# The first projections of a hybrid attention block: unused products ahead of the loads, gains inside the split of x, first weights on another queue, squares later

## The chip, the cores and the metric

One core of one Trainium2 chip. The metric is the device time of one execution in microseconds. A time of a kernel is the median of several executions; the profile is one further execution, recorded by the hardware profiler.

## The reference

One layer over 512 tokens of width 1024, all in float32, cut here to what the change touches:

```python
h = rms_norm(x, attn_norm)            # x * rsqrt(mean(x^2) + eps) * gain
proj = h @ w_in                       # q, k, v of attention A; cq, ckv, k_pe of attention B
sb_q, sb_k, sb_v, cq, ckv, k_pe = split(proj)
sb = stick_breaking_attention(sb_q, sb_k, sb_v)
q  = rms_norm(cq, cq_norm) @ w_uq
kv = rms_norm(ckv, ckv_norm) @ w_ukv
...                                   # attention B, output projection, PEER layer
```

cq has 384 columns, ckv 256; both are the "latents". The factor rsqrt(mean(x^2) + eps) belongs to a token, so the kernel multiplies x by the gain alone before the products and puts the factor on the products afterwards.

## The kernel before

Every float32 product is made of three fast ones: each operand is split into a high half (rounded to the float32r format by a copy on ScalarE) and a low half (the rest, by a subtraction on VectorE); high x high, high x low and low x high are summed in PSUM. `split` (lines 98 to 109) makes the halves, `mm3` (111 to 114) the three products, `copy_act` (93) is the copy on ScalarE. A weight tile of 128 columns is loaded raw, 512 KB on SP's queue (`raw_load`, line 117, three buffers), and split into two buffers of each half (`wparts`, 129).

x lies transposed: eight pieces xs of 128 rows by 512 tokens, 256 KB each. A projection of one weight tile (`project`, 304) is 8 pieces x 3 = 24 products of 512 columns into one of five PSUM banks.

The order of the work. A planner orders each engine's instructions by priority and by simulated times; `keep` holds instructions to the order written, `high_priority` moves some ahead. At the front two strings of steps are written by hand. ORD0 (line 62) is the order of the loads on SP: x0, the first weight tile w0, x1, x2, w1, x3 to x7, then the positions and a row of constants; the gains come before them (line 264). ORD1 (line 63) is the order of the steps on ScalarE, VectorE and GpSimd: for a piece k, gk is the multiplication by the gain on VectorE into a buffer xg (line 280), hk the high half hh on ScalarE (282), lk the low half hl on VectorE (284), sk a square of the raw piece on ScalarE (287) and its sum on GpSimd (`ssum`, 141 to 145); whk and wlk are the halves of weight tile k (291 and 293).

Behind these stand the tables of sines and cosines (295), the sum of squares over the partitions by a product with ones, psq (296), the token factor rs (`rsqrt`, 147 to 159: VectorE, twice ScalarE, three times VectorE), and its transposed column rcol (298 to 302). `lowrank` (310 to 331) does a latent: for each weight tile the projection, the multiplication by rs (318), a square and its sum; then two products with ones (323, 324: the sum of the earlier squares and the last square by itself), the latent's own factor, the multiplication by it (329) and a split. It runs for cq (tiles 0 to 2), then for ckv (tiles 3 and 4). After them come the value columns (337 to 357): two halves j of eight pieces kk, each piece a load of 136 KB, a split into one of four pairs of buffers (wvh, wvl), and 12 products of 272 columns into four PSUM banks pv of the same five; then the projections of q and k, the up-projections, and the attention heads.

Of the kernel before, what the change touches and what calls it, by code (L numbers as in the profile page):

```python
# [12 lines left out]
F32 = mybir.dt.float32  # L13
F32R = mybir.dt.float32r
BF16 = mybir.dt.bfloat16
# [8 lines left out]
P = 128  # L24
# [37 lines left out]
ORD0 = "x0 w0 x1 x2 w1 x3 x4 x5 x6 x7 t".split()  # L62
ORD1 = "g0 h0 l0 wh0 g1 h1 wl0 l1 s0 g2 s1 h2 g3 wh1 l2 h3 s2 g4 wl1 l3 h4 s3 g5 l4 h5 s4 g6 l5 h6 s5 g7 l6 h7 s6 l7 s7".split()
# [18 lines left out]
def hybrid_block(ctx: ExitStack, tc: tile.TileContext, A, out, out2, dbg=None, stop=None):  # L82
# [169 lines left out]
    with ExitStack() as pr:  # L252
# [10 lines left out]
        with tc.high_priority(offset=5 * AHEAD):  # L263
            nc.sync.dma_start(gains, A["gains"])
# [10 lines left out]
        wm, xg = {}, {}  # L275
        for step in ORD1:
            what, k = step[:-1], int(step[-1])
            if what == "g":
                xg[k] = pp.tile([P, S], F32, name="xg", tag="xg", bufs=2)
                keep(nc.vector.tensor_scalar(xg[k], xs[k], g_attn[:, k:k + 1], None, op0=OP.mult))  # L280
            elif what == "h":
                keep(copy_act(hh[:, k], xg[k]))
            elif what == "l":
                keep(nc.vector.tensor_sub(hl[:, k], xg[k], hh[:, k].bitcast(F32)))
# [10 lines left out]
        tables(pp, rows, posi)()  # L295
        nc.tensor.matmul(psq, ones, sqs, start=True, stop=True)
        rs = rsqrt(pp, psq, D, "x", [P, S])
        ptr = pz.tile([P, S], F32, name="ptr", tag="z1")
        for b in range(NB):
            nc.tensor.transpose(ptr[:, b * P:(b + 1) * P], rs[:, b * P:(b + 1) * P], ident)  # L300
        rcol = pp.tile([P, NB], F32, name="rcol")
        nc.vector.tensor_copy(rcol, ptr[:, ::P])
# [7 lines left out]
        def lowrank(first, n, width, gain, name):  # L310

            raw = pp.tile([P, n, S], F32, name=f"{name}_raw", tag="lr_raw", bufs=1)
            pv = pz.tile([P, S], F32, name=f"{name}_v", tag="z2")
            sqs = pp.tile([P, S], F32, name="sqs", tag="sqs", bufs=1)
            for m in range(n):
                w = wm[first + m] if first + m in wm else wload(A["wm"][first + m], KD, P, f"wm{first + m}")
                ps = project(w, f"{name}{m}")
                nc.vector.tensor_mul(raw[:, m], ps, rs)
                sq = pp.tile([P, S], F32, name="sq", tag="sq", bufs=2)
                nc.scalar.activation(sq, raw[:, m], AF.Square)  # L320
                if m < n - 1:
                    ssum(sqs, sq, m)
# [836 lines left out]
```

## Time and profile before

| | |
|---|---|
| runs of the kernel | 1634.97, 1636.81, 1643.74 us, median 1636.81 |
| profiled execution | 1636.4 us, span of its trace 1634.7 us |
| instructions | 24317 |
| busy: TensorE products, weight loads | 1543.7 us (94%), 1436.5 us (88%) |
| busy: VectorE, ScalarE, GpSimd | 1306.7 us (80%), 718.9 us (44%), 751.7 us (46%) |

PE is TensorE's products and PEld its weight loads, which overlap them; DVE is VectorE, ACT ScalarE, POOL GpSimd, SP the engine whose queue issues most loads. Times count from the start of the span. A line number is one of the kernel before; a helper's line stands for all who call it. In the rows, names such as `hl<-xg,hh` say what is written from what, and the bracket behind an instruction how long its engine stood idle before it and what ended that.

### The profile page before, as it was taken

The page shows a single profiled execution, that of the slowest core. Times are in us where ns is not written, and L with a number is a line of the kernel's source. Part 1 is how long each engine was busy: PE and PEld are TensorE (multiplying, and loading weights), DVE is VectorE, ACT ScalarE, POOL GpSimd, SP SyncE. Part 2 cuts the span into 40 slices and gives each one's busy share as a digit, 9 for nine tenths or more (in the row PEclk, how much of TensorE's full clock was granted, in tenths as well). Part 3 has the DMA queues.
Part 4 walks back from the last instruction along what each step waited for, and adds up shares of the span by engine and source line. Part 5 has one row for each costly group of instructions (what it writes and reads, how often), then busy time and mean ns, then how long its engine had stood idle before and what let it go on. Part 6 is the DMA issues. An engine that isn't in the chain of part 4 may idle for free.

```text
span 1634.7 us, 24317 instructions
## 1 busy us (share of the span) xinstructions
PE 1543.7 (94%) x8983; PEld 1436.5 (88%) x8983; DVE 1306.7 (80%) x2469; ACT 718.9 (44%) x1055; POOL 751.7 (46%) x655
## 2 busy tenths in 40 slices
PE   7998987979899999999999999989999998999996
PEld 4886665759899989989899999989999988999996
DVE  7557998889989899797857676778888888866667
ACT  5434775344444446666653333333333332333331
POOL 3003122434666741211136565655556677745454
PEclk9999998989899999999999999999999999999998
DMA  4330002423455567989899998999999999888776
GB/s 135 96 100 2 1 15 77 116 77 110 159 164 168 161 206 238 313 276 288 273 323 325 313 317 309 314 319 376 347 368 355 360 389 370 313 246 249 252 242 234
DMA packets 146551, 379.96 MB, mean 232 GB/s; under 512 B 11376, under 2 KB 64624, under 8 KB 146432
## 3 DMA queue, kind: packets, MB, share of 16 engines
q1 hardware_dynamic: 109568, 244.18, 44.7%
q0 software_dynamic: 36864, 134.23, 23.2%
q8 instruction: 70, 1.15, 0.3%
q14 instruction: 49, 0.40, 0.1%
HBM read 336.95 MB, written 41.42 MB: 231 GB/s over the span
## 4 chain that ended last, share of the span: by engine, by line
PE 54%; DVE 18%; DMA 14%; POOL 6%; issue 5%; ACT 3%; DVEq 0%; SPq 0%; ACTq 0%; POOLq 0%
PE pacc L113 9%; PE pacc L114 9%; PE pacc L112 9%; DMA row<-u,eidx 7%; PE psu L112 4%; PE psu L114 4%; PE psu L113 4%; POOL row L786 3%; DMA row<-v,eidx 3%; DMA u_r<-ut 3%; POOL tok L826 2%; PE pg L1037 2%; DVE u_l L106 2%; PE psx L113 1%; PE psx L114 1%
## 5 line engine op out<-in xcount | busy, mean ns | idle before, releaser
L113 PE MATMUL pacc<-cl,v_h 128*128 128x384 f32 x1024 | 345.3, 337 | 11.8 <-DVE cl L106 11.8
L112 PE MATMUL psu<-h2h,u_h 128*128 128x384 f32 x1024 | 349.9, 342 | 0.0
L114 PE MATMUL psu<-h2h,u_l 128*128 128x384 f32 x1024 | 345.7, 338 | 3.9 <-DVE u_l L106 3.9
L112 PE MATMUL pacc<-ch,v_h 128*128 128x384 f32 x1024 | 342.9, 336 | 1.9 <-ACT ch L94 1.9
L113 PE MATMUL psu<-h2l,u_h 128*128 128x384 f32 x1024 | 344.5, 336 | 0.0
L114 PE MATMUL pacc<-ch,v_l 128*128 128x384 f32 x1024 | 344.4, 336 | 0.0
L94 ACT ACTIVATE v_h<-v_r 128x1024 fp32r<-128x1024 f32 x128 | 135.9, 1062 | 330.6 <-PE pacc L113 224.8
L786 POOL DMA_INDIRECT row<-v,eidx x128 | 241.2, 1885 | 24.2 <-issue 24.0
L94 ACT ACTIVATE u_h<-u_r 128x1024 fp32r<-128x1024 f32 x128 | 135.6, 1059 | 228.1 <-PE psu L113 112.0
L106 DVE TENSOR_TENSOR v_l<-v_r,v_h 128x1024 fp32r<-128x1024 f32 x128 | 156.6, 1224 | 88.6 <-ACT v_h L94 87.4
L792 DVE CUSTOM_DVE_ANT_0 row<-row,h2n 128x1024 f32<-128x1024 f32 x128 | 158.1, 1241 | 67.4 <-DMA row<-u,eidx 66.7
L113 PEld LDWEIGHTS pacc<-cl,v_h 128*128 128x128 f32 x1024 | 194.1, 190 | 13.6 <-DVE cl L106 13.4
L114 PEld LDWEIGHTS psu<-h2h,u_l 128*128 128x128 f32 x1024 | 193.7, 189 | 5.6 <-DVE u_l L106 5.6
L112 PEld LDWEIGHTS pacc<-ch,v_h 128*128 128x128 f32 x1024 | 193.1, 189 | 2.2 <-ACT ch L94 2.2
L112 PEld LDWEIGHTS psu<-h2h,u_h 128*128 128x128 f32 x1024 | 194.1, 190 | 1.0 <-issue 0.5
L113 PEld LDWEIGHTS psu<-h2l,u_h 128*128 128x128 f32 x1024 | 194.1, 190 | 0.3
L114 PEld LDWEIGHTS pacc<-ch,v_l 128*128 128x128 f32 x1024 | 194.2, 190 | 0.0
L800 DVE SCALAR_TENSOR_TENSOR acc<-row,coef,acc 128x1024 f32<-128x1024 f32 x128 | 163.9, 1280 | 23.6 <-DMA row<-v,eidx 23.0
L826 POOL COPY tok<-u_l 1x1 f32<-1x1 f32 x90 | 56.8, 632 | 262.7 <-DVE u_l L106 262.5
L786 POOL DMA_INDIRECT row<-u,eidx x128 | 160.4, 1253 | 32.0 <-issue 25.2
L826 POOL COPY tok<-v_l 1x1 f32<-1x1 f32 x125 | 80.6, 645 | 197.1 <-DVE v_l L106 197.0
L106 DVE TENSOR_TENSOR u_l<-u_r,u_h 128x1024 fp32r<-128x1024 f32 x96 | 117.3, 1222 | 39.7 <-ACT u_h L94 34.3
(372 smaller groups left out, 2736.8 us busy)
## 6 DMA issues: line engine op xcount, KB each, us to landing
u_r<-ut SPq DMA_DIRECT2D x128, 512.0 KB
v_r<-v SPq DMA_DIRECT2D x128, 512.0 KB
gd<-gbuf SPq DMA_DIRECT2D x12, 2048.0 KB
gr<-gd SPq DMA_DIRECT2D x32, 768.0 KB
pd<-p SPq DMA_DIRECT2D x18, 768.0 KB
pr<-pd SPq DMA_DIRECT2D x18, 768.0 KB
wq_r<-wq SPq DMA_DIRECT2D x16, 512.0 KB
wqk_r<-wqk SPq DMA_DIRECT2D x8, 512.0 KB
```

Source lines behind the costliest of these rows:

```text
L94: return nc.scalar.activation(o, i, AF.Copy, scale=scale)
L106: b = nc.vector.tensor_sub(lo, src, hi.bitcast(F32))
L112: nc.tensor.matmul(ps, wh, xh, start=start, stop=False)
L113: nc.tensor.matmul(ps, wh, xl, start=False, stop=False)
L114: nc.tensor.matmul(ps, wl, xh, start=False, stop=stop)
L786: tc.keep_in_program_order(nc.gpsimd.indirect_dma_start(out=row, out_offset=None, in_=table, in_offset=bass.IndirectOffsetOnAxis(ap=eidx[: ...
L792: tc.keep_in_program_order(nc.vector.tensor_tensor_reduce(row, row, h2n, 1.0, 0.0, OP.mult, OP.add, pre[:, s:s + 1]))
L800: tc.keep_in_program_order(nc.vector.scalar_tensor_tensor(acc, row, coef[:, s:s + 1], acc, op0=OP.mult, op1=OP.add))
L826: tc.keep_in_program_order(nc.gpsimd.tensor_copy(tok, after[0:1, 0:1].bitcast(F32)))
L1037: nc.tensor.matmul(pg[:, u], ebf[:, t], egf[k][:, t], start=(k == 0), stop=(k == 1))
```

## The change

The loads of the gains and of the first weight tile go to ScalarE's queue, the tile in two halves of 256 KB. Thirteen products of a zeroed bf16 tile (`idle`, cleared on GpSimd) are written ahead of the projections; their PSUM tile `warm` is not read. The pass gk is gone: the high half is a copy with the gain as its scale, the low half one instruction that multiplies by the gain and subtracts. The first weight tile is split by halves. The squares of x come later in the order. The five projections of the latents are written before the parts that use rs: tiles 0 to 2, tables, psq, rs, then `lowrank_raw` of cq, tiles 3 and 4, the transposes, `lowrank_raw` of ckv; the rest of each latent's norm is written inside the value loop, before its pieces 1 and 6. Each latent's squares are all summed on GpSimd, with one product with ones for each latent.

```diff
--- before.py
+++ after.py
@@ -59,8 +59,9 @@
 EM0 = "ss0 lh0".split()
 EM = "lm0 ss0 lh1 lo-1 sw0 lw0 so0".split()
 ZB = 2
-ORD0 = "x0 w0 x1 x2 w1 x3 x4 x5 x6 x7 t".split()
-ORD1 = "g0 h0 l0 wh0 g1 h1 wl0 l1 s0 g2 s1 h2 g3 wh1 l2 h3 s2 g4 wl1 l3 h4 s3 g5 l4 h5 s4 g6 l5 h6 s5 g7 l6 h7 s6 l7 s7".split()
+ORD0 = "x0 x1 x2 w1 x3 x4 x5 x6 x7 t".split()
+ORD1 = "h0 wg0 l0 wg1 h1 wm0 l1 h2 wm1 l2 h3 l3 wh1 h4 wl1 l4 s0 h5 l5 s1 h6 l6 s2 h7 l7 s3 s4 s5 s6 s7".split()
+WARM = 13
 POOLQ = (1, 1)
 POOLU = range(0, 32)
 
@@ -261,7 +262,11 @@
         posi = pp.tile([P, NB], I32, name="posi")
         raws = {}
         with tc.high_priority(offset=5 * AHEAD):
-            nc.sync.dma_start(gains, A["gains"])
+
+            raws[0] = ws.tile([P, KD * P], F32, name="wm0_r", tag="wr", bufs=3)
+            nc.scalar.dma_start(gains, A["gains"])
+            for half in range(2):
+                nc.scalar.dma_start(raws[0][:, 512 * half:512 * half + 512], A["wm"][0][:, 4 * half:4 * half + 4])
             for step in ORD0:
                 if step == "t":
                     nc.sync.dma_start(posi, A["pos"])
@@ -272,16 +277,25 @@
                     nc.sync.dma_start(xs[int(step[1])], A["xT"][:, int(step[1])])
         psq = pz.tile([P, S], F32, name="psq", tag="z0")
         sqs = pp.tile([P, S], F32, name="sqs", tag="sqs", bufs=1)
-        wm, xg = {}, {}
+
+        idle = pp.tile([P, S], BF16, name="idle")
+        nc.gpsimd.memset(idle, 0.0)
+        warm = pz.tile([P, S], F32, name="warm", tag="z2")
+        for k in range(WARM):
+            nc.tensor.matmul(warm, idle[:, 0:P], idle, start=True, stop=True)
+        wm = {0: wparts(KD, P, "wm0")}
         for step in ORD1:
             what, k = step[:-1], int(step[-1])
-            if what == "g":
-                xg[k] = pp.tile([P, S], F32, name="xg", tag="xg", bufs=2)
-                keep(nc.vector.tensor_scalar(xg[k], xs[k], g_attn[:, k:k + 1], None, op0=OP.mult))
-            elif what == "h":
-                keep(copy_act(hh[:, k], xg[k]))
+            half = slice(512 * k, 512 * k + 512)
+            if what == "h":
+                keep(copy_act(hh[:, k], xs[k], scale=g_attn[:, k:k + 1]))
             elif what == "l":
-                keep(nc.vector.tensor_sub(hl[:, k], xg[k], hh[:, k].bitcast(F32)))
+                keep(nc.vector.scalar_tensor_tensor(hl[:, k], xs[k], g_attn[:, k:k + 1], hh[:, k].bitcast(F32),
+                                                    op0=OP.mult, op1=OP.subtract))
+            elif what == "wg":
+                keep(copy_act(wm[0][0][:, half], raws[0][:, half]))
+            elif what == "wm":
+                keep(nc.vector.tensor_sub(wm[0][1][:, half], raws[0][:, half], wm[0][0][:, half].bitcast(F32)))
             elif what == "s":
                 sq = pp.tile([P, S], F32, name="sq", tag="sq", bufs=2)
                 keep(nc.scalar.activation(sq, xs[k], AF.Square))
@@ -292,14 +306,6 @@
             else:
                 keep(nc.vector.tensor_sub(wm[k][1], raws[k], wm[k][0].bitcast(F32)))
         wm = {k: wm3d(w, P) for k, w in wm.items()}
-        tables(pp, rows, posi)()
-        nc.tensor.matmul(psq, ones, sqs, start=True, stop=True)
-        rs = rsqrt(pp, psq, D, "x", [P, S])
-        ptr = pz.tile([P, S], F32, name="ptr", tag="z1")
-        for b in range(NB):
-            nc.tensor.transpose(ptr[:, b * P:(b + 1) * P], rs[:, b * P:(b + 1) * P], ident)
-        rcol = pp.tile([P, NB], F32, name="rcol")
-        nc.vector.tensor_copy(rcol, ptr[:, ::P])
 
         def project(w, name):
             ps = pm.tile([P, S], F32, name=f"ps_{name}", tag="mm")
@@ -307,21 +313,22 @@
                 mm3(ps, w[0][:, kk], w[1][:, kk], hh[:, kk], hl[:, kk], kk == 0, kk == KD - 1)
             return ps
 
-        def lowrank(first, n, width, gain, name):
-
-            raw = pp.tile([P, n, S], F32, name=f"{name}_raw", tag="lr_raw", bufs=1)
-            pv = pz.tile([P, S], F32, name=f"{name}_v", tag="z2")
-            sqs = pp.tile([P, S], F32, name="sqs", tag="sqs", bufs=1)
+        def lowrank_raw(pss, name):
+
+            n = len(pss)
+            raw = pp.tile([P, n, S], F32, name=f"{name}_raw")
+            sqs = pp.tile([P, S], F32, name=f"sqs{name}")
             for m in range(n):
-                w = wm[first + m] if first + m in wm else wload(A["wm"][first + m], KD, P, f"wm{first + m}")
-                ps = project(w, f"{name}{m}")
-                nc.vector.tensor_mul(raw[:, m], ps, rs)
+                nc.vector.tensor_mul(raw[:, m], pss[m], rs)
                 sq = pp.tile([P, S], F32, name="sq", tag="sq", bufs=2)
                 nc.scalar.activation(sq, raw[:, m], AF.Square)
-                if m < n - 1:
-                    ssum(sqs, sq, m)
-            nc.tensor.matmul(pv, ones, sqs, start=True, stop=False)
-            nc.tensor.matmul(pv, ones, sq, start=False, stop=True)
+                ssum(sqs, sq, m)
+            return raw, sqs
+
+        def lowrank(raw, sqs, n, width, gain, name):
+
+            pv = pz.tile([P, S], F32, name=f"{name}_v", tag="z2")
+            nc.tensor.matmul(pv, ones, sqs, start=True, stop=True)
             r = rsqrt(pp, pv, width, name, [P, S])
             hi = lp.tile([P, n, S], F32R, name=f"{name}_h")
             lo = lp.tile([P, n, S], F32R, name=f"{name}_l")
@@ -330,8 +337,18 @@
                 split(hi[:, m], lo[:, m], raw[:, m])
             return hi, lo
 
-        cq = lowrank(0, 3, 384, g_cq, "cq")
-        ckv = lowrank(3, 2, 256, g_ckv, "ckv")
+        pss = [project(wm[m] if m in wm else wload(A["wm"][m], KD, P, f"wm{m}"), f"c{m}") for m in range(3)]
+        tables(pp, rows, posi)()
+        nc.tensor.matmul(psq, ones, sqs, start=True, stop=True)
+        rs = rsqrt(pp, psq, D, "x", [P, S])
+        cq = lowrank_raw(pss, "cq")
+        pss = [project(wload(A["wm"][m], KD, P, f"wm{m}"), f"c{m}") for m in (3, 4)]
+        ptr = pz.tile([P, S], F32, name="ptr", tag="z1")
+        for b in range(NB):
+            nc.tensor.transpose(ptr[:, b * P:(b + 1) * P], rs[:, b * P:(b + 1) * P], ident)
+        rcol = pp.tile([P, NB], F32, name="rcol")
+        nc.vector.tensor_copy(rcol, ptr[:, ::P])
+        ckv = lowrank_raw(pss, "ckv")
 
 
         with ExitStack() as wv_:
@@ -344,6 +361,11 @@
                     wvl = vp.tile([P, 272], F32R, name=f"wvl{j}{kk}", tag="wvl")
                     split(wvh, wvl, raw_load(A["wv"][:, kk, js], 272, f"wv{j}{kk}"))
                     st, sp = kk == 0, kk == KD - 1
+
+                    if (j, kk) == (0, 1):
+                        cq = lowrank(*cq, 3, 384, g_cq, "cq")
+                    if (j, kk) == (0, 6):
+                        ckv = lowrank(*ckv, 2, 256, g_ckv, "ckv")
                     for b in range(NB):
                         bs = slice(b * P, (b + 1) * P)
                         nc.tensor.matmul(pv[b], hh[:, kk, bs], wvh, start=st, stop=False)
```

## Rows read from the trace of the kernel before

**Rows 1.** The page, busy time: engine, busy us (share), instructions.
```profile
PE 1543.7 (94%) x8983; PEld 1436.5 (88%) x8983; DVE 1306.7 (80%) x2469; ACT 718.9 (44%) x1055; POOL 751.7 (46%) x655
```

**Rows 2.** Busy time by stage: length; PE, PEld, DVE, ACT, POOL (records); clock, DMA share, GB/s.
```profile
7.00:21.00 14.00, 11.89 (x24) 7.14 (x25) 11.81 (x18) 7.95 (x14) 7.67 (x6) 1.00 0.71 250
...
21.00:36.20 15.20, 13.41 (x57) 9.73 (x56) 13.85 (x30) 9.34 (x15) 4.23 (x3) 1.00 0.10 28
...
36.20:50.40 14.20, 12.87 (x53) 9.67 (x52) 11.16 (x18) 5.96 (x10) 2.33 (x2) 1.00 0.14 40
...
50.40:76.80 26.40, 26.21 (x195) 24.77 (x195) 12.58 (x23) 11.59 (x24) 0.61 (x1) 1.00 0.38 108
...
76.80:130.00 53.20, 53.20 (x245) 44.42 (x244) 29.48 (x45) 20.55 (x36) 2.86 (x5) 1.00 0.28 92
```

**Rows 3.** The chain of waits, 0 to 30 us: start us, us, what.
```profile
3.62 7.64 DMA xs<-xT
...
13.29 2.31 DVE wm_l L293
...
22.57 1.77 DVE hl L284
...
27.16 1.23 DVE wm_l L106
```

**Rows 4.** The timeline of PE: start us, us, engine, line, operation [idle before].
```profile
6.98 0.79 PE L112 MATMUL ps_cq<-hh,wm_h 128*128 128x512 f32 x1 [6.98 <-ACT wm_h L94]
...
20.06 0.63 PE L114 MATMUL ps_cq<-hh,wm_l 128*128 128x512 f32 x1
...
20.48 0.63 PE L112 MATMUL ps_cq<-hh,wm_h 128*128 128x512 f32 x1
...
29.70 0.39 PE L112 MATMUL ps_cq<-hh,wm_h 128*128 128x512 f32 x1
...
33.56 0.39 PE L114 MATMUL ps_cq<-hh,wm_l 128*128 128x512 f32 x1
...
39.96 1.13 PE L323 MATMUL cq_v<-sqs,ones 128*128 128x512 f32 x2 [1.33 <-POOL sqs L145]
...
40.92 1.02 PE L324 MATMUL cq_v<-sq,ones 128*128 128x512 f32 x2
...
50.44 0.28 PE L349 MATMUL pv<-wvh,hh 128*128 128x272 f32 x1
```

**Rows 5.** Groups by line, 0 to 50 us: what xcount | busy us, mean ns | idle.
```profile
L145 POOL TENSOR_TENSOR sqs<-sqs,sq 128x512 f32<-128x512 f32 x8 | 12.7, 1582 | 6.2 <-ACT sq L287 5.0 <-ACT sq L320 0.9
...
L284 DVE TENSOR_TENSOR hl<-xg,hh 128x512 fp32r<-128x512 f32 x8 | 8.7, 1093 | 0.7 <-ACT hh L94 0.7
...
L94 ACT ACTIVATE wm_h<-wm_r 128x1024 fp32r<-128x1024 f32 x5 | 5.3, 1056 | 2.4 <-PE ps_cq L113 2.2
...
L94 ACT ACTIVATE hh<-xg 128x512 fp32r<-128x512 f32 x8 | 5.0, 630 | 9.1 <-DVE xg L280 9.1
...
L280 DVE TENSOR_SCALAR xg<-xs,gains 128x512 f32<-128x512 f32 x8 | 4.8, 600 | 5.6 <-DMA xs<-xT 5.4
```

**Rows 6.** The timeline of the first 5 us: ACT, SP's queue, DVE.
```profile
0.81 1.28 ACT L94 ACT_TABLE_LOAD   x1 [0.81 <-PEq L1148]
...
1.26 0.42 SPq L272 DMA_DIRECT2D xs<-xT  x1
...
4.66 0.49 DVE L280 TENSOR_SCALAR xg<-xs,gains 128x512 f32<-128x512 f32 x1 [3.33 <-DMA xs<-xT]
```

**Rows 7.** Busy time around one pause of PE, columns as in the second group.
```profile
151.10:154.40 3.30, 0.02 (x1) 0.00 (x0) 2.59 (x7) 0.91 (x3) 1.71 (x3) 0.99 0.00 0
...
154.50:161.10 6.60, 5.81 (x13) 2.03 (x14) 5.49 (x14) 2.01 (x4) 0.00 (x0) 0.50 0.03 6
```

**Rows 8.** The waits, 0 to 80 us: who for whom: us, times, longest.
```profile
ACT wvh L94 <- PE pv L350: 4.8, 5, 1.1
```

**Rows 9.** The timeline of DVE: the last low halves of the first norm.
```profile
48.21 1.89 DVE L106 TENSOR_TENSOR cq_l<-cq_raw,cq_h 128x512 fp32r<-128x512 f32 x3
```

## The prediction

> **What bounds the kernel now.** I began with the busy times: TensorE is busy 94% of the span [rows 1], so time can be won only where TensorE stands idle or runs slowly. The busy time by stage says where. From 50.4 to 130 us TensorE is full, 26.21 of 26.40 us and 53.20 of 53.20, while the other engines are not [rows 2]; ScalarE's splits of the value weights even wait for TensorE to release their buffers [rows 8]. Whatever is won before 50 us therefore passes through this stretch as a plain shift. Before 50 us TensorE has gaps, and in 7 to 21 us it retires only 24 products in 14 us [rows 2].
>
> The chain of waits then names what holds TensorE in those first 30 us. It is the fourth piece of x until 11.36 us, and from there VectorE: the second tile's low halves, the last low half of x, the third tile's low halves [rows 3]. VectorE is slow there in two ways. It multiplies x by the gains in a pass of its own, eight times 0.600 us, and its eight low halves of x take 1.093 us on the mean [rows 5]. A pair of low weight halves takes 2.31 us at 13.29 but 1.23 us at 27.16, when GpSimd's sums are over [rows 3]; those sums are 1.58 us each [rows 5]. I read the stretching as a price of GpSimd running beside VectorE.
>
> The timeline of PE adds the clock. At 20 us two products start 0.42 us apart, from 29.70 to 33.56 seventeen steps take 3.86 us, 0.227 each [rows 4]. 512 columns in 0.42 us is the 1.2 GHz level, although the clock column prints 1.00 there [rows 2]; the first is the lower level, the second the 2.4 GHz one.
>
> **The change part by part.** My marker is the first value product, 50.44 us before [rows 4]. Ahead of it lie 120 products of the five tiles, the ones-products and four transposes.
>
> (a) *Loads.* On SP the issue of one load costs about 0.42 us, and x's first one starts at 1.26 us, behind the gains [rows 6]. With the gains and the first weights on ACT's queue, x0 issues some 0.45 us sooner and x3 two issues plus that sooner, 0.9 to 1.3 us. ACT gets three issues, 1.3 us, on top of its 1.28 us table load: free near 3.4 us, before x0 lands at 4.66 [rows 6]. If that cover were gone, 1.3 us. The traffic is the same. Bounds for the landing of x3: 10.1 us (the issue decides) to 11.4 (bandwidth decides, as the DMA share of 0.71 over 7 to 21 us suggests [rows 2]); I take 11.4. The Trainium skill, "Trainium Kernel Development and Optimization", Key Constraints, says that DMAs of the SP, ACT and POOL queues share the same 16 engines, so another queue saves issue time alone. By that rule the sum stays as it is; with bandwidth of its own for the second queue it would be about 1.3 us better.
>
> (b) *Unused products.* No row shows them. Thirteen of 512 columns at the low spacing of 0.42 us are 5.5 us; begun near 1.5 to 2 us they end near 7.0 to 7.5, or a little sooner if the clock rises among them. The first true product could then start near 5.7 but starts at 7.2, against 6.98 now [rows 4]. That costs nothing, because everything up to x3 waits for loads. What they can buy is the 2.4 GHz level. The clock fell after a pause of 3.30 us with one product in it, and 154.5 to 161.1 ran at 0.50 [rows 7]. The pauses I expect before x3 are 1 to 1.6 us, so I take the high level to hold. Bounds: nothing lost; or the low level from 13.1 to 20.9, where the present kernel still had it: 7.8 us hold 18 products instead of 34, and 16 x 0.227 = 3.7 us are lost.
>
> (c) *Norm's factors in the split.* Eight VectorE passes of 0.600 us go, and with each the step VectorE to ScalarE (its hand-over shows as ScalarE's 9.1 us of idling [rows 5]). The scaled copy on ScalarE I cost as the present 0.63 us copy, the fused low half as the fast present low half, 0.7 us.
>
> (d) *Order of ScalarE.* After x3: split h3 0.63, second tile's high halves 1.06, so the second tile's products can start at 11.4 + 1.7 = 13.1 us. Then four more splits and three squares of the same size, 7 x 0.63 = 4.4, so the last split ends near 17.5 and the last low half, beside GpSimd's sums at about 1.1 us, near 18.8. TensorE has by 13.1 done about 12 of the first two tiles' 48 products; the other 36 take 36 x 0.227 = 8.2 us, to 21.3, and their inputs are never late.
>
> (e) *Third tile.* Its split buffers are the first tile's, so its high halves follow that tile's last product near 19.4, 1.06 us, and its low halves would end at 21.8 by the 1.23 us price, at 22.9 by the 2.31 us one. The squares moved back put GpSimd's eight sums at about 14 to 27 us, just there, so I take 22.9. TensorE comes to the first low product at 21.75 and waits: +1.0 us, bounds 0 and 2.2 (a second stretched pair for the fourth tile).
>
> (f) *The norms of the latents* leave the path between the tiles. The idle of 1.33 us before the first one's ones-product goes, and its second ones-product, 0.96 us, with it [rows 4]. One per norm remains, both now among the value products, where formerly two of one norm stood: no difference there. The square sum of x and the four transposes remain, 0.96 and, by their columns, some 0.4 us. The three held sums of products keep three of five PSUM banks until the factor of x is known: last sum 27, the factor some 6 us later, 33 to 35 with the multiplications, before the value products need the banks at 39. Cover 4 us.
>
> *Sum.* From 13.1: 108 products x 0.227 = 24.5, plus 1.4, gives 39.0; the low halves' wait makes 40.0, and 0.5 us I allow for the value stage, which now holds two norm chains (between 0 and the second rival's price): 40.5 against 50.44, **10 us less**. The profiled execution took 1636.4 us around a span of 1634.7, so 1626.4; the median of the runs, 1636.81, lies 0.4 above it, so 1626.8. Its own range: best 39.0 less the 1.3 us of (a), 12.7 us won, 1624.1; worst 39.0 + 3.7 + 2.2 + 1.33 (a wait for the square sum, as now), 4.2 us won, 1632.6.
>
> **Rivals.**
> *The win shrinks in the front.* The clock stays low, or GpSimd's sums now stretch the weights' halves instead of x's: 4 to 7 us won, about 1631. For it: the stretched pair of [rows 3], and that the pauses between x0 and x3 come just after the unused products. Against it: those pauses are less than half of the one in [rows 7]. The Trainium skill, "GPSIMD Engine Reference" (its table of specs), has GpSimd's SBUF interfaces shared with VectorE when VectorE reads two SBUF inputs; the rows agree (1.23 against 2.31), and the fused low half still reads two.
> *The value stage takes it back.* The first norm's chain runs from 39.96 to 50.1 [rows 4, 9], and two such chains now share VectorE's queue with sixteen low halves of value weights. Four split pairs cover 4 x 26.21/16 = 6.6 us [rows 2], so each chain could hold TensorE 3.5 us: 7 of 10 given back, 1633.8. Against it: VectorE is busy 12.58 of 26.40 us in that stage [rows 2] and would have room.
> *Slower.* The order of each queue is planned by simulated times, and a front that is 10 us shorter may be followed by another order in the attention heads, where VectorE's chain holds TensorE already. One such pause costs 3.3 us and a low clock afterwards another 3.3 [rows 7], 6.6 together. One more leaves 3.4 us won, two make it 3.2 slower (1640), and from three, 1646, it is clearly slower. Against it: the full stretch up to 130 us hands over the same instructions.
> *The change does less than it says:* the unused products are put after the true ones. Then (b) falls to its 3.7 us, inside the first rival.
>
> **How the numbers follow.** A measurement of this kernel can tell about 0.5%, 8.2 us, from no change. Forecast 0.60, first rival 0.25, second 0.09, third 0.06. Of the forecast nearly all lies beyond 8.2 us, and what of it does not is made up by the first rival's better end: faster 0.60. The first two rivals lie within 8.2 us: 0.34. Slower 0.06, most of the third. The range takes the forecast's bounds, somewhat more gain below, and the second rival above: 1622.5 to 1634.5.
>
> **What would show it.** Right: the first value product near 40 us; steps of 0.23 us by 13 us; low halves of x near 0.7 us; no gain pass; TensorE full from there to 120 us and the end 10 us sooner. Wrong: steps of 0.42 us after 13 us; a wait of the third tile's first low product over 2 us; idle before value products for VectorE's low halves; new pauses in the heads. If the first value product comes at 40 and the end does not move, the shift was given back later.

## The result and the profile after

| | before | after |
|---|---|---|
| median of the runs (16 each) | 1635.58 us (1627.77 to 1643.74) | 1625.24 us (1620.51 to 1631.58) |
| ratio, 95% interval | | 0.9945 [0.9928, 0.9961] |
| profiled execution, span | 1636.4, 1634.7 us | 1627.63, 1625.9 us |
| first value product | 50.44 us | 45.23 us |
| first product of q and k | 77.05 us | 71.21 us |
| from there to the end of the span | 1557.6 us | 1554.7 us |

The change is faster by 0.55%, and the predicted 1626.8 us lies 1.6 us above the median. But the marker that the prediction named did not move as it said: the first value product came at 45.23 us, not near 40. The front (all that stands ahead of the first product of q and k) gave 5.8 us, somewhat more than half of the 10.3 us between the medians. The rest has no place in the front, and the experiments have to say what it is.

The page's busy line answers to [rows 1]; TensorE is busy 95%.

```profile
PE 1541.1 (95%) x8992; PEld 1434.1 (88%) x8992; DVE 1301.8 (80%) x2462; ACT 719.9 (44%) x1056; POOL 758.2 (47%) x658
```

Busy time by stage of the changed kernel, columns as in [rows 2]:

```profile
7.00:21.00 14.00, 9.86 (x29) 6.26 (x29) 11.79 (x14) 9.32 (x16) 7.05 (x5) 0.88 0.70 240
21.00:36.20 15.20, 14.65 (x55) 11.58 (x56) 10.65 (x25) 8.47 (x12) 4.70 (x3) 0.89 0.15 38
36.20:45.20 9.00, 9.00 (x42) 7.43 (x42) 5.59 (x11) 4.08 (x7) 3.53 (x4) 1.00 0.18 47
45.20:71.20 26.00, 26.00 (x199) 25.04 (x198) 18.54 (x33) 13.70 (x28) 1.49 (x2) 1.00 0.35 104
```

From 7 to 21 us TensorE retires 29 products instead of 24, far from the 36 and 12 that the prediction wanted by 21.3 us. From 21.55 us on, up to 71.2, it has no gap. The timeline of PE, columns as in [rows 4], tells where the first 21 us went:

```profile
1.39 5.01 PE L285 MATMUL warm<-idle 128*128 128x512 bf16 x13 [1.39 <-POOL idle L282]
...
10.06 0.49 PE L113 MATMUL ps_c<-hh,wm_h 128*128 128x512 f32 x1 [1.67 <-ACT hh L95]
...
12.51 0.63 PE L115 MATMUL ps_c<-hh,wm_l 128*128 128x512 f32 x1
12.94 0.63 PE L113 MATMUL ps_c<-hh,wm_h 128*128 128x512 f32 x1
...
21.55 0.50 PE L114 MATMUL ps_c<-hl,wm_h 128*128 128x512 f32 x1 [1.85 <-DVE hl L293]
...
33.09 1.02 PE L342 MATMUL psq<-sqs,ones 128*128 128x512 f32 x2
...
44.88 0.60 PE L348 MATMUL ptr<-ident,rr_x 128*128 128x128 f32 x4
45.23 0.37 PE L371 MATMUL pv<-wvh,hh 128*128 128x272 f32 x1
...
46.82 1.02 PE L331 MATMUL cq_v<-sqscq,ones 128*128 128x512 f32 x2
```

The unused products run from 1.39 to 6.40 us. TensorE still waits for x1's split until 10.06 and for the last low half of x until 21.55. From 12.5 to 15.5 us its products stand 0.43 us apart. The square sum, the transposes and the latent's ones-product come without an idle time before them; the 1.33 us of [rows 4] are gone.

The clock column shows the fall now, twice (length; PE, PEld, DVE, ACT, POOL; clock, DMA share, GB/s): 0.50 is the 1.2 GHz level.

```profile
13.00:15.00 2.00, 2.00 (x6) 1.59 (x5) 2.00 (x3) 2.00 (x5) 1.34 (x2) 0.50 0.96 289
...
23.00:25.00 2.00, 2.00 (x6) 1.63 (x5) 1.82 (x2) 1.19 (x3) 1.19 (x1) 0.50 0.00 0
```

VectorE's timeline shows what the last low half stood behind, and ScalarE's why the splits of x0 and x1 were late:

```profile
13.77 2.79 DVE L293 SCALAR_TENSOR_TENSOR hl<-xs,gains,hh 128x512 fp32r<-128x512 f32 x2
16.48 1.31 DVE L225 CAST identb<-ident 128x128 bf16<-128x128 f32 x1
17.71 0.74 DVE L293 SCALAR_TENSOR_TENSOR hl<-xs,gains,hh 128x512 fp32r<-128x512 f32 x1
18.37 1.31 DVE L226 TENSOR_SCALAR ntri<-tri 128x128 fp32r<-128x128 f32 x1
19.61 0.21 DVE L228 TENSOR_SCALAR causal<-tri 128x128 bf16<-128x128 f32 x1
19.74 1.75 DVE L293 SCALAR_TENSOR_TENSOR hl<-xs,gains,hh 128x512 fp32r<-128x512 f32 x1
...
23.18 1.23 DVE L107 TENSOR_TENSOR wm_l<-wm_r,wm_h 128x1024 fp32r<-128x1024 f32 x1 [1.69 <-ACT wm_h L95]
```

```profile
4.36 1.28 ACT L95 ACT_TABLE_LOAD   x1 [4.36 <-DMA xs<-xT]
...
8.77 0.63 ACT L95 ACTIVATE wm_h<-wm_r 128x512 fp32r<-128x512 f32 x1 [1.66 <-DMA wm_r<-wm]
9.30 1.93 ACT L95 ACTIVATE hh<-xs,gains 128x512 fp32r<-128x512 f32 x3
```

x1 itself was there at 6.3 us (issued at 1.25 us on SP, 5.0 us to its landing); its split stands in ScalarE's order behind that of the first tile's second half, which landed at 8.75. Two small constants, identb and ntri, stand between the last low halves of x; each takes 1.31 us, while causal, of the same 128 x 128, takes 0.21. The groups by line, columns as in [rows 5], say who runs beside them: GpSimd's sums.

```profile
L146 POOL TENSOR_TENSOR sqs<-sqs,sq 128x512 f32<-128x512 f32 x7 | 10.8, 1543 | 1.9 <-ACT sq L301 1.5
...
L293 DVE SCALAR_TENSOR_TENSOR hl<-xs,gains,hh 128x512 fp32r<-128x512 f32 x8 | 8.2, 1043 | 7.2 <-ACT hh L95 7.2
```

The gain pass of [rows 5] is gone, but the mean low half is as slow as before, 1.043 against 1.093 us. ScalarE's wait for the value products' buffers, 4.8 us in [rows 8], is now this:

```profile
ACT wvh L95 <- PE pv L372: 1.9, 3, 1.1
```

### The profile page after: what moved, and what is told of

It is laid out like the page before. It is cut to its first block, busy times and chain, and to the rows that moved or that the text cites. A ratio compares the mean times of both kernels' runs of the same rounds, so it can differ in the third digit from the quotient of the medians.

```text
span 1625.9 us, 24331 instructions
## 1 busy us (share of the span) xinstructions
PE 1541.1 (95%) x8992; PEld 1434.1 (88%) x8992; DVE 1301.8 (80%) x2462; ACT 719.9 (44%) x1056; POOL 758.2 (47%) x658
## 3 DMA queue, kind: packets, MB, share of 16 engines
q8 instruction: 70, 1.15, 0.3%
## 4 chain that ended last, share of the span: by engine, by line
PE 64%; DVE 16%; DMA 9%; POOL 4%; issue 3%; ACT 3%; another core or an unknown queue 0%; DVEq 0%; ACTq 0%; POOLq 0%
PE pacc L114 9%; PE pacc L115 9%; PE pacc L113 9%; PE psu L113 7%; PE psu L115 6%; PE psu L114 6%; DMA row<-u,eidx 5%; PE pg L1059 2%; POOL row L808 2%; DMA u_r<-ut 2%; DMA row<-v,eidx 2%; POOL tok L848 1%; PE psx L114 1%; PE psx L115 1%; DVE r L668 1%
## 5 line engine op out<-in xcount | busy, mean ns | idle before, releaser
L808 POOL DMA_INDIRECT row<-v,eidx x128 | 244.6, 1911 | 24.4 <-issue 23.5
L822 DVE SCALAR_TENSOR_TENSOR acc<-row,coef,acc 128x1024 f32<-128x1024 f32 x128 | 163.7, 1279 | 22.8 <-DMA row<-v,eidx 22.6
L848 POOL COPY tok<-v_l 1x1 f32<-1x1 f32 x125 | 77.1, 617 | 196.7 <-DVE v_l L107 196.6
```

Source lines behind the costliest of these rows:

```text
L808: tc.keep_in_program_order(nc.gpsimd.indirect_dma_start(out=row, out_offset=None, in_=table, in_offset=bass.IndirectOffsetOnAxis(ap=eidx[: ...
L822: tc.keep_in_program_order(nc.vector.scalar_tensor_tensor(acc, row, coef[:, s:s + 1], acc, op0=OP.mult, op1=OP.add))
L848: tc.keep_in_program_order(nc.gpsimd.tensor_copy(tok, after[0:1, 0:1].bitcast(F32)))
```

## The experiments

Twelve kernels ran, in three groups, each group on one chip beside 33 to 35 runs of the kernel before. "Gain in the front" is 77.05 us less the first q/k product of the profiled execution; "rest" is that execution's span behind that product. From 46 us behind the first q/k product on, and from that product on for TensorE and GpSimd, every engine has the same instructions in the same order in all these kernels; what differs there is time alone. Each place is that of one execution: two executions of one kernel lie 0.3 us (changed) and 0.6 us (before) apart at the first q/k product.

| kernel | first value product | first q/k product | gain in the front | rest | median (before) | ratio, 95% |
|---|---|---|---|---|---|---|
| before again | 50.1 | 76.5 | 0.6 | 1555.2 | 1632.39 (1632.85) | 0.9995 [0.9968, 1.0021] |
| changed again | 44.9 | 70.9 | 6.2 | 1552.7 | 1625.74 (1633.03) | 0.9970 [0.9950, 0.9991] |
| late norms alone | 44.7 | 70.7 | 6.4 | 1554.1 | 1628.83 (1630.53) | 0.9980 [0.9952, 1.0009] |
| gains in the split alone | 47.5 | 74.1 | 3.0 | 1554.7 | 1629.58 (1633.03) | 0.9977 [0.9951, 1.0003] |
| all but the late norms | 48.1 | 74.5 | 2.6 | 1548.1 | 1625.02 (1633.03) | 0.9963 [0.9941, 0.9984] |
| no unused products | 44.9 | 70.9 | 6.2 | 1556.7 | 1627.92 (1630.53) | 0.9968 [0.9942, 0.9995] |
| first weights on SP | 42.2 | 69.3 | 7.8 | 1560.4 | 1623.26 (1630.53) | 0.9956 [0.9933, 0.9979] |
| squares last | 40.6 | 68.7 | 8.4 | 1547.4 | 1619.05 (1630.53) | 0.9933 [0.9908, 0.9958] |
| squares last, weights on SP | 42.0 | 70.0 | 7.1 | 1557.5 | 1629.28 (1633.03) | 0.9991 [0.9970, 1.0013] |
| second tile ahead | 43.4 | 69.4 | 7.7 | 1554.2 | 1623.63 (1632.85) | 0.9958 [0.9931, 0.9985] |
| squares last, norm later | 41.0 | 67.0 | 10.1 | 1555.8 | 1615.87 (1632.85) | 0.9909 [0.9880, 0.9937] |
| squares last, no unused products | 41.9 | 70.4 | 6.7 | 1549.0 | 1624.72 (1632.85) | 0.9951 [0.9926, 0.9977] |

**Is the rest of the gain real?** Two kernels ran unchanged, the one after and the one before.

> The changed kernel itself once more, on the same chip as the three runs beside it. Theory A (the front gives 5.9 us and hands it on; behind the first q and k product every engine's order is the same as before, and what the profiled pair showed beyond the front, 2.9 us, is spread from run to run): first q and k product at 71.2 within 0.3 us, the span behind it anywhere from 1547 to 1561 us, the ratio 0.994 to 0.998. Rival F (the shift itself shortens the work behind): the span behind the first q and k product below 1555 us again and a ratio below 0.994.

> The kernel before against itself. Theory (behind the first query/key product the time wanders by itself, with the same instructions in the same order): first query/key product at 77.0 to 77.2 us, the stretch behind it anywhere from 1548 to 1561 us, ratio between 0.997 and 1.003 with 1 in it. Rival (the stretch behind is settled by the kernel, and its 1557.6 us is before's own): 1557 to 1558.5 us behind the first query/key product.

The changed kernel again gained 6.2 us in the front, but by its ratio 4.9 us in all (1.5 to 8.2), where the first comparison gave 9.0 (6.4 to 11.8). The kernel before, against itself, had 76.5 us for its first q/k product, 0.5 under what was expected, and 1555.2 us behind it, 2.4 us less than in its first profile. So the rest wanders by over 2 us with the kernel unchanged. Over the twelve, the gain in the front is 6.1 us on the mean and the gain by the ratios, taken of their medians of before, also 6.1; a straight line through the twelve pairs has a slope of 1.0 (correlation 0.70). Nine of the twelve ratios hold their front's gain inside the interval and one at its edge; outside are "squares last, weights on SP" (1.5 us, up to 4.9, against 7.1) and "squares last, norm later" (14.9 us, from 10.3, against 10.1). The first comparison's 6.4 to 11.8 does not hold its front's 5.8 either. So what is won before the first q/k product reaches the end, one for one as far as a spread of some 4 us in each comparison lets it be seen. The 10.3 us between the medians are best read as the front's 5.8 and such a spread.

**Which part won?** Each part alone.

> The kernel before with one part of the change alone: the five projections ahead of the token factor, the latents' norms inside the value loop. Theory A (this removes the pauses of 1.05 and 1.33 us and two ones-products of 0.96 us each, of which one is moved behind the marker; the first 25 us are as before): the first value product at 46 to 47.5 us against 50.4 before, the first product of the q and k projections at 73 to 74 against 77.1, the time 3 to 4 us less than before, so that more than half of the front's 5.8 us comes from this part. Rival E (the front's 5.8 us comes from the first 25 us, and the value stage pays for the two norm chains): the first q and k product within 1.5 us of 77.

```diff
 (the kernel before, its loads, splits and ORD1 untouched)
-        cq = lowrank(0, 3, 384, g_cq, "cq")
-        ckv = lowrank(3, 2, 256, g_ckv, "ckv")
+        pss = [project(...) for m in range(3)]
...
+                    if (j, kk) == (0, 1):
+                        cq = lowrank(*cq, 3, 384, g_cq, "cq")
```

All of PE's waits of this kernel up to 80 us (who for whom: us, times, longest):

```profile
PE ps_c L112 <- ACT wm_h L94: 7.0, 1, 7.0
PE ps_c L113 <- DVE hl L284: 1.7, 2, 1.0
PE ps_c L114 <- DVE wm_l L293: 0.2, 1, 0.2
```

The late norms alone gave 6.4 us in the front, more than expected and as much as the whole change. Gone from the front are the idle before the latent's ones-products (1.33 us), these two themselves, and a wait that the prediction had not counted, that of the transposes for x's factor, in the kernel before

```profile
34.99 0.66 PE L300 MATMUL ptr<-ident,rr_x 128*128 128x128 f32 x4 [1.05 <-DVE rr_x L158]
```

The waits for low halves shrank too, from 2.3 to 1.7 us; TensorE is without gaps from 23.5 us instead of 24.4. That is no work of the edit as far as the trace tells: x3 was there at 10.37 us in this execution, against 11.36 and 11.23 in the two of the kernel before, and the edit touches none of these loads.

> The kernel before with one part alone: the gain inside the two halves of x, no pass of its own. Theory A (VectorE loses eight passes of 0.6 us, but GpSimd's sums then run beside the low halves, and the late token factor and norms keep their pauses on TensorE): the last low half of x ends at 20 to 22.5 us instead of 24.3, the first value product comes at 48.5 to 50.5 against 50.4, the time 0 to 2 us less than before. Rival G (the passes set the front): first value product at 46.5 or earlier, 4 us.

```diff
-ORD1 = "g0 h0 l0 wh0 g1 h1 wl0 l1 s0 g2 s1 h2 ...
+ORD1 = "h0 l0 wh0 h1 wl0 l1 s0 s1 h2 wh1 l2 h3 ...
-                keep(copy_act(hh[:, k], xg[k]))
+                keep(copy_act(hh[:, k], xs[k], scale=g_attn[:, k:k + 1]))
-                keep(nc.vector.tensor_sub(hl[:, k], xg[k], hh[:, k].bitcast(F32)))
+                keep(nc.vector.scalar_tensor_tensor(hl[:, k], xs[k], ...
```

Gains in the split alone gave 3.0 us, a microsecond more than expected and less than the rival. VectorE's five last low halves took 8.56 us in a row from 13.08 us, 1.71 each beside the sums, so the queue was shorter and its pieces longer.

> The changed kernel with the norms back in their old place: token factor and tables ahead of the projections, both latents' norms between the tiles. Theory A (all the rest of the change brings nothing by itself, as the late norms alone brought the first q and k product to 70.7 us, earlier than the whole change): first value product at 49 to 51.5 us, first q and k product at 76 to 78, time within 2 us of before. Rival H (the two halves of the change share one slack, so that each alone brings nearly the whole): first q and k product at 73 or earlier.

```diff
-        cq = lowrank_raw(pss, "cq")
+        cq = lowrank(0, 3, 384, g_cq, "cq")
...
-                    if (j, kk) == (0, 1):
-                        cq = lowrank(*cq, 3, 384, g_cq, "cq")
```

All but the late norms gave 2.6 us, with the waits that the late norms remove all there again: 0.33 us for the transposes, 1.25 and 0.26 for the ones-products. 6.4 and 2.6 do not add up to 5.8. The new front's wait for x's last low half is no reason, for it is 1.85 us in this kernel too (to 20.55 us). Some 0.8 us is that the late norms found less to remove behind the new front: 0.33 us of waiting instead of 1.05, 1.25 instead of 1.33. About 2 us more go with loads that no edit touched: in this execution the first tile's second half was there at 7.75 us, a microsecond before that of the changed kernel (8.77), and all later splits of x with it; in "late norms alone" x3 came 1.0 us sooner. By its ratio this kernel gained more than its front did, 6.0 us (2.6 to 9.6), at the edge of its interval.

**What did the unused products and the other queue do?**

> The changed kernel without its 13 unused products. Theory A (the loads and VectorE's last low halves of x, stretched by GpSimd's sums, set the front; the clock matters only at its edges): the products from 7 us on stand 0.42 us apart until about 15 us, where the changed kernel ran fast only from 7 to 12; the waits for the low halves swallow nearly all of that, so the first value product comes at 45 to 46.5 us against 45.2 and the time is 0 to 1 us above the changed kernel's. Rival B (the unused products carry the win): the first value product falls back towards 48 to 50 us and the time to 3 us or more above the changed kernel's.

```diff
-WARM = 13
+WARM = 0
```

The front came out the same, 70.9 against 70.9 in the repeated run. ScalarE's split of the first tile's second half, and TensorE's products without the unused ones:

```profile
9.78 0.63 ACT L95 ACTIVATE wm_h<-wm_r 128x512 fp32r<-128x512 f32 x1 [2.98 <-DMA wm_r<-wm]
```

```profile
13.73 0.63 PE L115 MATMUL ps_c<-hh,wm_l 128*128 128x512 f32 x1
14.16 0.48 PE L113 MATMUL ps_c<-hh,wm_h 128*128 128x512 f32 x1
14.48 0.39 PE L114 MATMUL ps_c<-hl,wm_h 128*128 128x512 f32 x1
```

The steps become short at 14.2 us, earlier than with them (15.5). With them the products at 7.49 and 11.42 us took 0.39 us already, but from 12.5 us, behind the pauses of 1.67 us for x1 and 0.30 for a low half, the lower level was back. The run sets no price on the products, for the loads differ too: the second half landed a microsecond later here (9.78 us against 8.77 and 8.45), and x's low halves with it, the last one ready at 22.5 us; but behind that last wait the steps stayed at 0.23 us, where the changed kernel lost 1.6. It shows that the win does not hang on the unused products.

> The changed kernel with the two halves of the first weight tile back on SP's queue behind x0; the gains stay on ScalarE's queue. Theory A (the second queue shares the engines with the first, and the second half, which lands only near 8.7 us behind the later pieces of x, holds ScalarE's queue ahead of x1's high half): the second half lands by 6.5 us, x1's high half starts at 7 to 8 us instead of 9.3, the pieces of x behind it 0 to 2 us earlier; first value product 44 to 45.2 us, time 0 to 1.2 us less. Rival D (the second queue brings the weights sooner and its loss would be felt): the first true product later than 7.2 us and the first value product later than 45.5.

```diff
-ORD0 = "x0 x1 x2 w1 x3 x4 x5 x6 x7 t".split()
+ORD0 = "x0 w0 x1 x2 w1 x3 x4 x5 x6 x7 t".split()
-            for half in range(2):
-                nc.scalar.dma_start(raws[0][...], ...)
+                elif step == "w0":
+                    for half in range(2):
+                        nc.sync.dma_start(raws[0][...], ...)
```

With the first weights back on SP behind x0, the front gained 1.6 to 1.9 us more, which neither expectation foresaw. ScalarE's timeline, and VectorE's:

```profile
6.00 1.13 ACT L95 ACTIVATE wm_h<-wm_r 128x512 fp32r<-128x512 f32 x2
9.22 1.34 ACT L95 ACTIVATE hh<-xs,gains 128x512 fp32r<-128x512 f32 x2 [2.09 <-DMA xs<-xT]
```

```profile
11.91 0.22 DVE L225 CAST identb<-ident 128x128 bf16<-128x128 f32 x1
12.04 0.22 DVE L226 TENSOR_SCALAR ntri<-tri 128x128 fp32r<-128x128 f32 x1
...
14.65 5.24 DVE L294 SCALAR_TENSOR_TENSOR hl<-xs,gains,hh 128x512 fp32r<-128x512 f32 x4
```

Both halves are split by 7.13 us, where from the other queue the second landed at 8.75; and x1's split starts at 9.22 against 9.30, then for want of x1 and not of its place in the order: x1 landed at 9.2 us behind the tile, at 6.3 beside it. The Trainium skill, "Trainium Kernel Development and Optimization", Key Constraints, has all queues on the same 16 engines, interleaving; the trace agrees, for what the tile won (its second half at 5.4 instead of 8.75 us) x1 lost. x3's split even began later, at 11.80 instead of some 10.5 us. So the gain is not that of the queue. It stands in VectorE's order, which the planner changed with the edit: the constants now come before the sums, 0.22 us each, and the last low half is ready at 19.89 us instead of 21.49, though each of the last four still takes 1.3 us beside the sums; nor do the steps become long again behind it.

**Were the squares late enough?**

> The changed kernel with all eight squares of x behind the last low half. Theory A (GpSimd's sums beside VectorE stretch the low halves of x 5 to 7 and the constants set among them, 4 to 5 us in all): each of those low halves takes 0.75 us, the last one ends near 17 to 18 us instead of 21.5, TensorE's wait of 1.85 us before it goes, and the first value product comes at 41 to 42.5 us instead of 45.2; the time falls by 3 to 4 us below the changed kernel's. Rival C (the sums now stretch the third tile's low halves by as much, and the wait moves there): the first value product stays within 1 us of 45.2.

```diff
-ORD1 = "... wl1 l4 s0 h5 l5 s1 h6 l6 s2 h7 l7 s3 s4 s5 s6 s7".split()
+ORD1 = "... wl1 l4 h5 l5 h6 l6 h7 l7 s0 s1 s2 s3 s4 s5 s6 s7".split()
```

VectorE's last four low halves, GpSimd's sums and TensorE's longest wait behind them:

```profile
13.77 3.08 DVE L293 SCALAR_TENSOR_TENSOR hl<-xs,gains,hh 128x512 fp32r<-128x512 f32 x4
```

```profile
16.40 10.75 POOL L146 TENSOR_TENSOR sqs<-sqs,sq 128x512 f32<-128x512 f32 x7
```

```profile
43.51 1.13 PE L331 MATMUL cq_v<-sqscq,ones 128*128 128x512 f32 x2 [1.18 <-POOL sqscq L146]
```

The same low halves take 0.75 us each and are through at 16.85 us instead of 21.49; the sums start beside the last of them, and the two slow constants come behind them. The edit moves both, so that it does not part the two. The first value product comes at 40.6 us, where the prediction had put it. The q/k product gains only 2.5 us of these 4.6, since the latent's ones-product now waits 1.18 us for GpSimd and another 0.5 us goes to a value piece.

> The changed kernel with the squares behind the last low half of x and with the first weight tile's halves back on SP's queue behind x0. Theory A (both gains are of the same wait, TensorE's for the last low halves and the third tile, so they add only in part): first value product at 39.5 to 41.5 us, where each alone gave 40.6 and 42.2, and first q and k product at 67.5 to 69; time 8 to 11 us below before. Rival J (they add in full): first value product at 38 us or earlier.

The edits of the last two together did not add up: 70.0 us, behind either alone and outside the expectation. x3's split begins at 11.50 us here and the last low half is ready at 17.44, 0.6 later than with the squares last alone. TensorE then waits 0.25 and 0.52 us for the fourth tile's halves at 30 us and again 1.00 us for the ones-product, and by the ratio this kernel hardly gained.

> The kernel with the squares last, and the norm of the first latent issued before the fourth value piece instead of the second. Theory (the 1.18 us in which the norm's product waited for GpSimd's sums was left because the cover of one value piece is too short when the projections end at 40.6 us): that wait is gone, the value stage takes 26.5 to 27.2 us instead of 28.1, the first query/key product lies at 67.3 to 68.0 us against 68.7. Rival (the norm has its own due time: cq's scaled halves are wanted by the first query product): the first query/key product waits for them by over 1 us and lies at 68.7 us or later.

```diff
-                    if (j, kk) == (0, 1):
+                    if (j, kk) == (0, 3):
```

(on top of the squares last.) The timeline of PE:

```profile
41.03 0.37 PE L371 MATMUL pv<-wvh,hh 128*128 128x272 f32 x1
...
45.61 1.02 PE L331 MATMUL cq_v<-sqscq,ones 128*128 128x512 f32 x2
...
66.99 0.40 PE L113 MATMUL ps_qk<-hh,wqk_h 128*128 128x512 f32 x1
```

The wait is gone and nothing waits for the norm later: the value stage takes 26.0 us. It is the best version that ran, 0.9909 of the kernel before, ahead of the changed kernel too (its two ratios: 0.9945 and 0.9970), though the intervals of the first of these and of this one overlap.

> The kernel with the squares last, without the unused products. There TensorE waits little once the first tile runs, so that a faster clock at the start could pay. Theory (the clock falls again at 12 us with the waits for x's split whatever was multiplied before, so they give nothing): first value product at 40.3 to 41.0 us, as with them (40.6). Rival (with the split no longer late the products gave about a microsecond): 41.4 us or later.

```diff
-WARM = 13
+WARM = 0
```

(also with the squares last.) 41.9 us is on the rival's side of the line, but not by the rival's mechanism. The kernel that differs by the products alone is "squares last". TensorE's steps become short at 15.2 us here, against 14.0 there, but by the product of x's square sum both are level, 28.36 and 28.38 us. The loss lies later, in these waits of PE and behind this order of ScalarE:

```profile
29.76 0.50 PE L113 MATMUL ps_c<-hh,wm_h 128*128 128x512 f32 x1 [0.38 <-ACT wm_h L95]
...
31.02 0.50 PE L115 MATMUL ps_c<-hh,wm_l 128*128 128x512 f32 x1 [0.53 <-DVE wm_l L107]
```

```profile
24.94 1.28 ACT L203 ACT_TABLE_LOAD   x1
...
28.66 1.04 ACT L95 ACTIVATE wm_h<-wm_r 128x1024 fp32r<-128x1024 f32 x1
```

The planner put the fourth tile's high halves behind the sines (28.66 us; with the unused products they came at 24.91). From the square sum's product to the third one behind it TensorE takes 2.66 us, there 1.33; that is the whole difference to 40.6. Both expectations were about the clock, and the planner's order decided.

**Did TensorE's order hold ready work back?** In the changed kernel about nine of the second tile's products stand ahead of the first tile's last ones.

> The changed kernel with TensorE's order of the first three tiles written out: thirteen parts of the second tile (instead of about nine products) may run ahead of the first tile's last parts, so that ready work no longer stands behind a product that waits for the split of x. Theory (the order held ready products back): no wait for a low half of x over 0.5 us on TensorE, some 42 products of the first two tiles done by 21.5 us instead of 29, but in this order the split of the third weight tile comes behind all squares on ScalarE, so the third tile starts at 25 to 26 us and the first value product lies at 42.5 to 44.5 us against 45.2. Rival (the order is indifferent, the split of x sets the pace): the first value product stays at 45.0 us or later, and the wait only moves to the third tile's first product.

```diff
+        for step in "00 01 02 03 10 11 04 12 13 05 14 06 15 07 16 17 20 21 22 23 24 25 26 27".split():
+            m, kk = int(step[0]), int(step[1])
+            for i, (w, x) in enumerate(((wm[m][0], hh), (wm[m][0], hl), (wm[m][1], hh))):
+                keep(nc.tensor.matmul(pss[m], w[:, kk], x[:, kk], ...))
```

```profile
21.16 0.50 PE L345 MATMUL ps_c<-hl,wm_h 128*128 128x512 f32 x1 [0.65 <-DVE hl L293]
...
23.92 0.50 PE L345 MATMUL ps_c<-hh,wm_h 128*128 128x512 f32 x1 [0.65 <-ACT wm_h L95]
...
26.12 0.50 PE L345 MATMUL ps_c<-hh,wm_l 128*128 128x512 f32 x1 [1.47 <-DVE wm_l L107]
```

The wait for the last low half falls from 1.85 to 0.65 us, a little over the half microsecond expected, though that low half is ready only 0.4 us sooner (21.10). Of the work freed, 1.47 us is lost again at the third tile's low halves, which took 2.17 us beside the sums. The front gains 1.8 us: order and lateness both counted.

## Why the prediction was right, and where it was not

The side and the total came out, the total by luck: the front gave 5.8 us instead of 10, which is what the first rival had said ("4 to 7 us won"), and the spread behind it added some 4 us to the first comparison. By its steps:

**(a) Loads.** The gain allowed for came on x3: its split began at some 10.5 us instead of 11.88 and was over by 11.2, sooner than the landing at 11.4 taken. The cover failed. ScalarE was not free near 3.4 us: its table load waited for x0 and ran from 4.36 to 5.64 us, all 1.28 us on the path of x0's split. And the second half of the first tile, on the other queue, was split at 8.77 us ahead of x1 in ScalarE's order, where x1 had been there since 6.3. What this part came to in all stays open: the gain of "first weights on SP" is that of the constants' place.

**(b) Unused products.** "I take the high level to hold" was wrong. The clock fell at 12 us and again at 22.6 us; some eight steps each time at 0.43 instead of 0.23 us, about 1.6 us twice. No run shows that the products bought anything by the clock; the one kernel that lost without them ("squares last") lost by the planner's order.

**(c) Gains in the split** came as priced: the split took 0.71 us instead of 0.63, the fused low half 0.75 where GpSimd was still, and 3.0 us were won by it alone.

**(d) Order of ScalarE** is the step that failed. Its own queue kept time: the last split ended at 16.2 us, before the 17.5 predicted. "The last low half near 18.8" and "their inputs are never late" did not hold, for VectorE's queue was summed without the two constants in it, 1.31 us each, and without all the sums' stretching: 21.49 us. So TensorE had 29 products behind it at 21.5 us instead of 48; 19 x 0.227 = 4.3 us, of which the six slow steps behind 13.1 us, of (b), are 1.2. With the second fall of the clock, 1.6 us, and without the wait of (e), -1.0, the predicted 40.0 becomes 44.9 against the measured 45.23. "Squares last" takes both causes away and gives 40.6; "first weights on SP" takes the constants alone, against a later x3, and gives 42.2. The Trainium skill, "GPSIMD Engine Reference" (its table of specs), on GpSimd's interfaces being shared with VectorE at two SBUF inputs, agrees with the fused low half (0.75 alone, 1.75 beside a sum); the constants, of one input, were stretched as much, 0.21 to 1.31. For these the sentence has only a 2-port mode, and no row tells whether they ran in it.

**(e) Third tile.** The wait of 1.0 us (by its own numbers 22.9 less 21.75, 1.15) did not come. Its high halves began at 22.09, late because the first tile was, and its low halves fell mostly between two of GpSimd's sums, 1.23 us.

**(f) The norms** held and were undersized: 2.3 us were named, 6.4 measured for the part alone: the idle 1.33, the transposes' wait 1.05, the two ones-products 1.9, 0.9 of low halves that came earlier with x3, 0.6 in the value stage, and 0.6 more; the cause of the last two stays open. The cover of 4 us for x's factor sufficed; no transposes waited.

**Second rival:** the value stage took nothing back, 26.0 us against 26.6, where the prediction allowed 0.5 more. With the squares last it did, 28.1, for a cover of one piece is too short when the projections end at 40.6 us. **Third rival:** the order behind the front did not change, and the time there fell by 2.9 us; repeated runs put that within the spread.

## What to carry to other kernels

When a queue is shortened, sum the whole queue of the engine that feeds the bottleneck, with small constants in it and at the price they have beside GpSimd, and not only the instructions of the change. Work that stretches another engine is moved behind the last piece that the bottleneck waits for; a half-way place lets it run beside just those. And a forecast of half a per cent is tested at a marker in the trace first: here the end wandered by as much as the gain. Where a planner sets the order, one edited line can move others: before a gain is put down to the edit, look for what else moved, as the constants did here.

## What was not expected of the hardware

**The spread goes with the granted clock.** In the 33, 35 and 35 runs of the kernel before that went with the three groups, the span falls by 0.8, 1.1 and 1.3 us for each 0.001 of mean granted clock (correlation -0.51, -0.78, -0.82). One stretch, first of the kernel before, then of all but the late norms:

```profile
280.00:380.00 100.00, 90.81 (x381) 72.56 (x380) 88.10 (x184) 39.18 (x58) 39.32 (x29) 0.91 0.33 97
```

```profile
280.00:380.00 100.00, 90.70 (x426) 74.16 (x425) 90.26 (x200) 44.72 (x67) 40.90 (x32) 0.98 0.32 100
```

TensorE is busy as long, but at 0.91 it retires 381 products and at 0.98 it retires 426. The order is not strict: "first weights on SP" retired 397 in this stretch at 0.90. That the clock is the cause, and what settles it in one execution, was not tried.

**The clock's column at the start.** Without unused products it prints 1.00 in the stretch from 11 to 13 us, where the steps are 0.43 us; with them it prints 0.84 there and 0.50 from 13 to 15. The spacing of the steps is the safer reading.

**What stood before the clock's fall.** In the changed kernel the steps were 0.23 us at 11.2 and 0.43 from 12.5 us, behind a pause of 1.67 us that ended at 10.06; and 0.43 again from 22.6 us, behind one of 1.85. Without the late norms they were 0.43 from 10.4 us, behind pauses of 0.77 and 0.29 us. But without the unused products a pause of 1.62 us, up to 22.59, was followed by steps of 0.23 us. The kernel before had lost the upper level after 3.30 us [rows 7]. The length of one pause does not sort these cases.
